# A fused low-rank update: one load in place of two, a sum moved ahead of a turn, and other waits for two stores

## The chip, the cores and the metric

The kernel runs on one core of a Trainium2 chip. The time is that of one execution on the device, in microseconds (us). The core has five engines that run side by side and meet through semaphores: TensorE (PE in the profile; PEld is its loading of weights), VectorE (DVE), ScalarE (ACT), GpSimd (POOL) and SyncE (SP), which here only issues transfers. Sixteen DMA engines move the data between the chip's memory (DRAM) and the core's SBUF; TensorE writes to PSUM.

## The reference

```python
def reference(x, A, B, scale):
    lora = np.matmul(np.matmul(x, A), B)
    return (x + scale * lora).astype(np.float32)
```

`x` is 16 x 512 x 768 in fp32, `A` is 768 x 16, `B` is 16 x 768, `scale` is 0.5. So 8192 rows of 768 numbers are read, each gets a small low-rank correction, and 8192 rows are written: 25.2 MB in, 25.2 MB out.

## The kernel before

**Tiles, parts, groups.** The 8192 rows are 64 tiles of 128 rows. A tile of fp32 is 393,216 bytes. For transfers the tiles lie in five parts of 9, 7, 16, 16 and 16 tiles (`PARTS`, L14); within a part each of the 128 partitions holds neighbouring rows, so that a partition's share of a transfer is one contiguous run. `LOADS` (L106) lists the loads as (part, first tile, tiles). The buffer `x_sb` has room for 48 tiles; the last 16 tiles reuse the places of the first 16, so the loads of part 4 wait until stores 0 and 1 are done. Results are summed in place in `x_sb` and stored from there, one store for each part (`STORES`, L128).

**Groups.** Computation goes by eight groups of 8 tiles (`GROUP`). Group g goes through these steps:

1. *narrowed* (L186): the 8 tiles are cast from fp32 to fp16 into `xn`, the first four by ScalarE, the last four by GpSimd. It waits for the load, and for `s_taken`, which says that TensorE has begun on the group before.
2. *turned* (L248): VectorE transposes all 8 tiles in blocks of 32 x 32, from `xn` to `xt`.
3. *projected* (L278): 24 matmuls form x times A in PSUM (`ps_yt`). They run in two halves of 12; the last one raises `s_y`.
4. ScalarE multiplies the result by the scale, in four instructions, and spreads it into `y_bd` (L238).
5. *raised* (L293): for each of four pairs of tiles TensorE multiplies by B, four matmuls, into one of two PSUM buffers (`lora_ps`). Raising pair p of a group needs the buffer that was last read for the pair two before it (`s_free`). The last matmul of a pair raises `s_lora`.
6. *summed* (L252): VectorE adds a pair's PSUM buffer to its two tiles in `x_sb`.

**The order on each engine is written out.** TensorE's loop (L324) does, for group g: raise pairs 0 and 1; wait for the turn of group g+1; project its first half; raise pairs 2 and 3; project the second half. VectorE (L265) does the turn of group g+1 and then the four sums of group g. ScalarE (L232) does its cast of group g+1 and then the multiplies of group g. GpSimd does its casts one after the other.

**SyncE's order** (L136). It issues the loads of parts 0 to 3 at the start, then `summed(0)`: it waits for the sums of group 1, and passes on to TensorE that the last pair's buffer is free (`s_free[3]`; VectorE signals `s_sum` there instead). Then it waits until `s_lora` counts ten pairs, that is until group 2's first two pairs are raised, and issues stores 0 and 1. When store 0 is done it issues the first load of part 4, when store 1 is done the second. Store 2 waits for the sums of group 3 and for `s_raise`, which counts the first raising matmul of each group, to reach 6. Stores 3 and 4 wait for the sums of groups 5 and 7. All transfers go through this one queue.

Of the kernel before, what the change touches and what calls it, by code (L numbers as in the profile page):

```python
# [13 lines left out]
PARTS = [9, 7, 16, 16, 16]  # L14


GROUP = 8
# [11 lines left out]
def kernel(  # L29
# [19 lines left out]
    NG = sum(PARTS) // GROUP  # L49
    PAIRS = GROUP // 2  # L50
# [32 lines left out]
    def sem(name):  # L83
        sems.append(nc.alloc_semaphore(name))
        return sems[-1]
# [10 lines left out]
    def memory(t2, i, s, n):  # L96
        S = PARTS[i]
        return t2[ds(parts[i], S * P), :].rearrange("(p s) d -> p s d", s=S)[:, ds(s, n), :]

    def held(i, s, n):  # L100
        return tiles(where.index((i, s)), n)

    def tiles(t, n):
        return x_all[:, ds(t % ROOM, n), :]

    LOADS = [  # L106
        (0, 0, 2), (0, 2, 7), (1, 0, 7), (2, 0, 8), (2, 8, 8), (3, 0, 16), (4, 0, 8), (4, 8, 8)
    ]
    s_load = [sem(f"s_load{k}") for k in range(len(LOADS))]

    def load_of(t):
        i, s = where[t]
        return next(k for k, ld in enumerate(LOADS) if ld[0] == i and ld[1] <= s < ld[1] + ld[2])
# [6 lines left out]
    s_y, s_spread, s_lora = sem("s_y"), sem("s_spread"), sem("s_lora")  # L120

    s_free = [sem(f"s_free{p}") for p in range(PAIRS)]
    s_out0, s_out1, s_raise = sem("s_out0"), sem("s_out1"), sem("s_raise")

    s_sum, s_out = sem("s_sum"), sem("s_out")

# [1 line left out]
    STORES = [(0, 0, 9), (1, 0, 7), (2, 0, 16), (3, 0, 16), (4, 0, 16)]  # L128

    STORED = [where.index((i, s + n - 1)) // GROUP for i, s, n in STORES]  # L130
    assert STORED[0] == STORED[1]

    section = ExitStack()
    section.enter_context(tc.tile_critical(no_gpsimd_drain=True))  # L134
# [1 line left out]
    def on_sync(e):  # L136
        def load(k):
            ld = LOADS[k]
            e.dma_start(out=held(*ld), in_=memory(x2, *ld)).then_inc(s_load[k], 16)  # L139

        def summed(k):
            e.wait_ge(s_sum, sorted(set(STORED)).index(STORED[k]) + 1)
            if STORED[k] + 1 < NG:

                e.sem_inc(s_free[PAIRS - 1], 1)

        def store(k, done):
            st = STORES[k]
            e.dma_start(out=memory(out2, *st), in_=held(*st)).then_inc(done, 16)

        load(0)
        load(1)
        e.wait_ge(s_ready, 1)
        blocks = A.rearrange("(c e) r -> c (e r)", e=64)
        for c in range(SETS):
            e.dma_start(
                out=a_rows[c : SET * SET : SET, :], in_=blocks[ds(c * SET, SET), :]
            ).then_inc(s_a, 16)
        e.wait_ge(s_brows, 1)
        e.dma_start(out=b_rows[0 : R * APART : APART, :], in_=B).then_inc(s_b, 16)  # L160
        for k in range(2, len(LOADS) - 2):
            load(k)

        for p in range(2, PAIRS):
            e.sem_inc(s_free[p], 1)
        summed(0)


        e.wait_ge(s_lora, 2 * PAIRS + 2)
        store(0, s_out0)  # L170
        store(1, s_out1)
        e.wait_ge(s_out0, 16)
        load(len(LOADS) - 2)
        e.wait_ge(s_out1, 16)
        load(len(LOADS) - 1)
        for k in range(2, len(STORES)):
            summed(k)
            if k == 2:


                e.wait_ge(s_raise, 6)
            store(k, s_out)

    here = set()
# [1 line left out]
    def narrowed(e, copy, g, first, n=SUB):  # L186
        t = g * GROUP + first
        for k in dict.fromkeys(load_of(t + k) for k in range(n)):
            if (e, k) not in here:
                here.add((e, k))  # L190
                e.wait_ge(s_load[k], 16)
        if g:
            e.wait_ge(s_taken, g)
        ins = copy(out=xn[:, ds(first, n), :], in_=tiles(t, n))  # L194

        ins.then_inc(s_narrow if g else s_first if first else s_a, 1)
# [30 lines left out]
    def on_scalar(e):  # L227
        narrowed(e, e.copy, 0, SUB // 2, SUB // 2)
        narrowed(e, e.copy, 0, SUB)
        e.wait_ge(s_bp, 1)  # L230
        e.copy(out=b_mm, in_=lora[0][:, 0, :]).then_inc(s_bm, 1)  # L231
        for g in range(NG):  # L232
            if g + 1 < NG:
                narrowed(e, e.copy, g + 1, 0)
            e.wait_ge(s_y, g + 1)
            for b in range(NQ):
                q = ds(b * Q, Q)
                last = e.mul(out=y_bd[q, :, q], in_=y_ps[q, :, :], mul=sc)  # L238
            last.then_inc(s_spread, 1)

    def on_vector(e):
        e.wait_ge(s_a, SETS * 16 + 1)
        e.transpose(  # L243
            out=a_t[0:Q].rearrange("i k r c -> i (k r) c"),
            in_=a_rows[0:Q].rearrange("c (i k r) -> c (k r) i", k=2, r=R),
        ).then_inc(s_ready, 1)

        def turned(first, n):  # L248
            ts = [v[:, ds(first, n), :].bitcast(fp32) for v in (xt, xn)]
            return e.transpose(out=ts[0], in_=ts[1])  # L250

        def summed(g, p):  # L252
            xs = tiles(g * GROUP + 2 * p, 2)
            e.wait_ge(s_lora, g * PAIRS + p + 1)
            ins = e.tensor_tensor(out=xs, in0=xs, in1=lora[p % 2], op=mybir.AluOpType.add)  # L255
            if p + 1 == PAIRS and g in STORED:
                ins.then_inc(s_sum, 1)
            elif g + 1 < NG or p + 2 < PAIRS:
                ins.then_inc(s_free[p], 1)

        for h in range(2):
            e.wait_ge(s_first, h + 1)
            ins = turned(h * SUB, SUB)
        ins.then_inc(s_turned, 1)
        for g in range(NG):  # L265
            if g + 1 < NG:
                e.wait_ge(s_y, g + 1)
                e.wait_ge(s_narrow, 2 * (g + 1))  # L268
                turned(0, GROUP).then_inc(s_turned, 1)
            for p in range(PAIRS):  # L270
                summed(g, p)

    def on_tensor(e):


        xv = xt.rearrange("p s (c j k) -> p s c j k", c=NC, k=2)

        def projected(first, last):  # L278
            for m in range(first, last):
                c, k = divmod(m, 2)  # L280
                mm = e.matmul(  # L281
                    y_ps, w_bd[:, c, k, :], xv[:, :, c, :, k],
                    start=(m == 0), stop=(m == MMS - 1),
                )
                if m == 0:
                    mm.then_inc(s_turned, -1)
                if m == 1:

                    mm.then_inc(s_taken, 1)
                if m == MMS - 1:  # L290
                    mm.then_inc(s_y, 1)

        def raised(p):  # L293
            if p == 0:
                e.wait_ge(s_spread, 1)
            free = s_free[(p + 2) % PAIRS]
            e.wait_ge(free, 1)
            t = lora[p % 2]
            mms = []
            for k in range(2):  # L300
                for n0, w in ((0, 512), (512, 256)) if k == 0 else ((0, 256), (256, 512)):
                    mms.append(e.matmul(  # L302
                        t[:, k, ds(n0, w)], y_bd[:, 2 * p + k, :], b_mm[:, ds(n0, w)],
                        start=True, stop=True,
                    ))
            if p == 0:
                mms[0].then_inc(s_raise, 1)
                mms[2].then_inc(s_spread, -1)
            mms[1].then_inc(free, -1)
            mms[-1].then_inc(s_lora, 1)  # L310

        e.wait_ge(s_pick, 2)
        e.wait_ge(s_bh, 1)
        for n0, w in ((0, 512), (512, 256)):
            last = e.matmul(  # L315
                lora[0][:, 0, ds(n0, w)], pick.rearrange("p b r -> p (b r)"),
                b_half[:, ds(n0, w)], start=True, stop=True,
            )
        last.then_inc(s_bp, 1)
        e.wait_ge(s_w, 1 + NQ)  # L320
        e.wait_ge(s_turned, 1)
        projected(0, MMS)
        e.wait_ge(s_bm, 1)
        with e.Fori(0, NG - 1):  # L324
            raised(0)
            raised(1)
            e.wait_ge(s_turned, 1)
            projected(0, MMS // 2)
            raised(2)
            raised(3)  # L330
            projected(MMS // 2, MMS)
        for p in range(PAIRS):
            raised(p)

    on_sync(nc.sync)
    on_gpsimd(nc.gpsimd)
    on_scalar(nc.scalar)
    on_vector(nc.vector)
    on_tensor(nc.tensor)

# [43 lines left out]
```

## Time and profile before

| | us |
|---|---|
| median of 3 runs (123.42 to 123.6) | 123.47 |
| the profiled execution | 123.43 |
| its span, first to last instruction | 121.6 |
| VectorE busy | 81.7 |
| TensorE matmuls busy | 49.8 |
| ScalarE busy | 37.4 |
| GpSimd busy | 28.4 |

How to read it: the span is cut into 40 slices of 3.04 us, with a digit for the busy share in tenths. The granted clock of TensorE stands there as well. A group of instructions is named by its line, engine, operation, and what it writes and reads. In the timeline each row has the start, the duration, the engine, the line, the count, and in brackets the idle time ahead of it with what ended it. Rows of SP give the moment of issue of a transfer, not its duration. The transfers put through 50.43 MB in 1928 packets, a mean of 415 GB/s over the span. Every sum of a pair takes 1.7 us on VectorE, every turn of a full group 3.4, every cast of four tiles 2.75 on either engine.

### The profile page before, as it was taken

How to read it: one execution, taken by the hardware profiler on the slowest of the kernel's cores; microseconds unless marked ns; L12 is line 12 of the kernel's file. 1: busy time of each engine (PE TensorE's matmuls, PEld its weight loads, DVE VectorE, ACT ScalarE, POOL GpSimd, SP SyncE). 2: the span in 40 equal slices, each digit the busy share in tenths (PEclk: the TensorE clock that was granted, in tenths of full speed). 3: DMA queues.
4: the chain of work that ended last, by engine and by line, in shares of the span. 5: the costliest groups of instructions: out<-in, count | busy, mean ns of one | idle time of the engine just before them, and what ended most of it. 6: DMA issues, size and time to landing. Idle time of an engine off the chain costs nothing.

```text
span 121.6 us, 884 instructions
## 1 busy us (share of the span) xinstructions
PE 49.8 (41%) x322; PEld 29.2 (24%) x322; DVE 81.7 (67%) x42; ACT 37.4 (31%) x43; POOL 28.4 (23%) x24
## 2 busy tenths in 40 slices
PE   0000209487457547746745734774674320000000
PEld 0000006253223424424423322442442110000000
DVE  0000970599999999999999989999995990000000
ACT  4000967626408312735340093643004000000000
POOL 7730567126009002605300080620000000000000
PEclk9999999999999999999999999999999995555555
DMA  3999999999999897999999999998999899899890
GB/s 63 437 431 457 446 398 469 404 420 469 437 517 420 356 517 336 427 421 410 446 416 436 428 428 485 420 517 372 404 517 404 372 517 404 372 517 404 372 517 0
DMA packets 1928, 50.43 MB, mean 415 GB/s; under 512 B 236, under 2 KB 236, under 8 KB 392
## 3 DMA queue, kind: packets, MB, share of 16 engines
q1 hardware_dynamic: 1928, 50.43, 97.0%
HBM read 25.26 MB, written 25.17 MB: 415 GB/s over the span
## 4 chain that ended last, share of the span: by engine, by line
DVE 33%; DMA 29%; PE 9%; ACT 6%; POOL 2%; issue 2%; SPq 0%; DVEq 0%
DVE x_sb L255 21%; DMA x_sb<-in_x_dram 20%; DVE xt L250 12%; DMA out_dram<-x_sb 9%; PE ps_yt L281 6%; ACT xn L194 3%; PE lora_ps L302 3%; ACT y_bd L238 2%; POOL xn L194 2%; SPq L139 0%; SPq L379 0%; DVEq L268 0%; SPq L134 0%
## 5 line engine op out<-in xcount | busy, mean ns | idle before, releaser
L255 DVE TENSOR_TENSOR x_sb<-x_sb,lora_ps 128x1536 f32<-128x1536 f32 x32 | 53.7, 1735 | 1.4 <-PE lora_ps L302 1.4
L194 ACT CAST xn<-x_sb 128x3072 f16<-128x3072 f32 (+1 forms) x9 | 23.4, 2609 | 35.9 <-DMA x_sb<-in_x_dram 24.8
L302 PE MATMUL lora_ps<-b_mm,y_bd 128*128 128x512 f16 (+1 forms) x128 | 25.0, 328 | 22.6 <-ACT y_bd L238 14.3
L194 POOL CAST xn<-x_sb 128x3072 f16<-128x3072 f32 (+1 forms) x8 | 20.7, 2586 | 43.9 <-DMA x_sb<-in_x_dram 24.6
L250 DVE STREAM_TRANSPOSE xt<-xn 128x3072 f32<-128x3072 f32 (+1 forms) x9 | 27.1, 3006 | 5.3 <-PE ps_yt L281 4.4
L281 PE MATMUL ps_yt<-xt,w_bd 128*128 128x256 f16 x192 | 25.2, 282 | 12.2 <-DVE xt L250 12.2
L281 PEld LDWEIGHTS ps_yt<-xt,w_bd 128*128 128x128 f16 x192 | 18.5, 99 | 19.7 <-issue 15.4
L302 PEld LDWEIGHTS lora_ps<-b_mm,y_bd 128*128 128x128 f16 x128 | 10.6, 97 | 35.5 <-ACT y_bd L238 16.6
L238 ACT ACTIVATE y_bd<-ps_yt 32x256 f16<-32x256 f32 x32 | 12.0, 374 | 18.7 <-PE ps_yt L281 18.4
L243 DVE STREAM_TRANSPOSE a_t<-a_rows 32x1024 f32<-32x1024 f32 x1 | 2.0, 1955 | 12.2 <-DMA a_rows<-in_A_dram 12.2
L315 PE MATMUL lora_ps<-b_half,pick 128*128 128x512 f16 (+1 forms) x2 | 0.8, 500 | 13.5 <-POOL b_half L212 13.5
L315 PEld LDWEIGHTS lora_ps<-b_half,pick 128*128 128x128 f16 x2 | 0.1, 105 | 13.5 <-issue 13.5
L212 POOL CAST b_half<-b_rows 128x768 f16<-128x768 f32 x1 | 0.8, 827 | 5.5 <-DMA b_rows<-in_B_dram 5.5
L220 POOL COPY w_bd<-w_one 32x384 f16<-32x384 f16 x4 | 2.0, 500 | 0.2
L194 ACT ACT_TABLE_LOAD x1 | 1.3, 1283 | 0.9 <-SPq L134 0.9
L202 POOL MEMSET w_bd<- 128x1536 f32 x1 | 1.4, 1372 | 0.0
L214 POOL CAST w_one<-a_t 32x384 f16<-32x384 f32 x1 | 0.9, 857 | 0.9 <-DVE a_t L243 0.9
L199 POOL MEMSET a_rows<- 32x1024 f32 x1 | 0.9, 941 | 0.5 <-SPq L134 0.5
L231 ACT CAST b_mm<-lora_ps 128x768 f16<-128x768 f32 x1 | 0.8, 798 | 0.0
L200 POOL MEMSET b_rows<- 128x768 f32 x1 | 0.7, 728 | 0.0
L203 POOL MEMSET y_bd<- 128x512 f32 x1 | 0.5, 514 | 0.0
L205 POOL TENSOR_SCALAR_AFFINE_SELECT pick<-pick 128x128 f16<-128x128 f16 x1 | 0.3, 298 | 0.0
(5 smaller groups left out, 0.6 us busy)
## 6 DMA issues: line engine op xcount, KB each, us to landing
out_dram<-x_sb SPq DMA_DIRECT2D x3, 6144.0 KB, 20.1
x_sb<-in_x_dram SPq DMA_DIRECT2D x4, 3072.0 KB, 17.6
x_sb<-in_x_dram SPq DMA_DIRECT2D x1, 6144.0 KB, 41.6
x_sb<-in_x_dram SPq DMA_DIRECT2D x2, 2688.0 KB, 12.4
out_dram<-x_sb SPq DMA_DIRECT2D x1, 3456.0 KB, 11.5
out_dram<-x_sb SPq DMA_DIRECT2D x1, 2688.0 KB, 17.7
x_sb<-in_x_dram SPq DMA_DIRECT2D x1, 768.0 KB, 4.5
a_rows<-in_A_dram SPq DMA_DIRECT2D x3, 16.0 KB
```

Of the source, the lines that this page charges most:

```text
L194: ins = copy(out=xn[:, ds(first, n), :], in_=tiles(t, n))
L199: e.memset(a_rows[0:Q], 0.0).then_inc(s_ready, 1)
L202: e.memset(w_bd.rearrange("p c k m -> p (c k m)").bitcast(fp32), 0.0)
L214: e.tensor_copy(out=w_one.rearrange("i (c e) k r -> i c e (k r)", c=SETS), in_=a_t[0:Q].rearrange("i k r (e c) -> i c e (k r)", c=SET)[:, ...
L220: e.tensor_copy(out=w_bd[ds(b * Q, Q), :, :, ds(b * Q, R)], in_=w_one).then_inc(s_w, 1)
L238: last = e.mul(out=y_bd[q, :, q], in_=y_ps[q, :, :], mul=sc)
L243: e.transpose(out=a_t[0:Q].rearrange("i k r c -> i (k r) c"), in_=a_rows[0:Q].rearrange("c (i k r) -> c (k r) i", k=2, r=R),).then_inc(s_r ...
L250: return e.transpose(out=ts[0], in_=ts[1])
L255: ins = e.tensor_tensor(out=xs, in0=xs, in1=lora[p % 2], op=mybir.AluOpType.add)
L281: mm = e.matmul(y_ps, w_bd[:, c, k, :], xv[:, :, c, :, k], start=(m == 0), stop=(m == MMS - 1),)
L302: mms.append(e.matmul(t[:, k, ds(n0, w)], y_bd[:, 2 * p + k, :], b_mm[:, ds(n0, w)], start=True, stop=True,))
L315: last = e.matmul(lora[0][:, 0, ds(n0, w)], pick.rearrange("p b r -> p (b r)"), b_half[:, ds(n0, w)], start=True, stop=True,)
```

## The change

Five edits, made together:

- Part 2 is loaded by one transfer of 16 tiles in place of two of 8, on one semaphore. Groups 2 and 3 both lie in part 2.
- VectorE: in the turn for group 1 it sums the first pair of group 1 ahead of turning group 2, and the other three pairs behind it. In all other groups the order is as before.
- ScalarE: for g = 1 the cast of group 2 comes behind the multiplies of group 1 and no longer ahead of them.
- SyncE: store 0 waits for the projection of group 2 (`s_y` at 3) and no longer for the sums of group 1 and ten raised pairs. Its nine tiles are group 0 and the first tile of group 1's first pair, whose sum now stands ahead of group 2's turn. Then come the wait for group 1's sums with the passing on of `s_free[3]`, and store 1.
- SyncE: store 2 waits for the projection of group 5 (`s_y` at 6) and no longer for the first raising matmul of group 5. The semaphore `s_raise` is gone.

```diff
     LOADS = [
-        (0, 0, 2), (0, 2, 7), (1, 0, 7), (2, 0, 8), (2, 8, 8), (3, 0, 16), (4, 0, 8), (4, 8, 8)
+        (0, 0, 2), (0, 2, 7), (1, 0, 7), (2, 0, 16), (3, 0, 16), (4, 0, 8), (4, 8, 8)
     ]
...
         for p in range(2, PAIRS):
             e.sem_inc(s_free[p], 1)
-        summed(0)
-        e.wait_ge(s_lora, 2 * PAIRS + 2)
+        e.wait_ge(s_y, 3)
         store(0, s_out0)
+        summed(1)
         store(1, s_out1)
...
             if k == 2:
-                e.wait_ge(s_raise, 6)
+                e.wait_ge(s_y, 6)
             store(k, s_out)
...
         for g in range(NG):
-            if g + 1 < NG:
+            if g + 1 < NG and g != 1:
                 narrowed(e, e.copy, g + 1, 0)
             e.wait_ge(s_y, g + 1)
...
             last.then_inc(s_spread, 1)
+            if g == 1:
+                narrowed(e, e.copy, g + 1, 0)
...
         for g in range(NG):
+            ahead = 1 if g == 1 else 0
+            for p in range(ahead):
+                summed(g, p)
             if g + 1 < NG:
                 e.wait_ge(s_y, g + 1)
                 e.wait_ge(s_narrow, 2 * (g + 1))
                 turned(0, GROUP).then_inc(s_turned, 1)
-            for p in range(PAIRS):
+            for p in range(ahead, PAIRS):
                 summed(g, p)
...
             if p == 0:
-                mms[0].then_inc(s_raise, 1)
                 mms[2].then_inc(s_spread, -1)
```

More of the change, by code (lines that the diff above doesn't have):

```diff
@@ L122 @@
     s_free = [sem(f"s_free{p}") for p in range(PAIRS)]
-    s_out0, s_out1, s_raise = sem("s_out0"), sem("s_out1"), sem("s_raise")
+    s_out0, s_out1 = sem("s_out0"), sem("s_out1")
     s_sum, s_out = sem("s_sum"), sem("s_out")
@@ L130 @@
     STORED = [where.index((i, s + n - 1)) // GROUP for i, s, n in STORES]
-    assert STORED[0] == STORED[1]
+    assert STORED[0] == STORED[1] == 1 and PARTS[0] <= GROUP + 2
     section = ExitStack()
```

## The prediction

> **What bounds the kernel now.** I first read the busy shares by slice on the profile's page, to see which resource is never idle, and the queue's total.
>
> ```profile
> span 121.6 us, 884 instructions
> DVE  0000970599999999999999989999995990000000
> DMA  3999999999999897999999999998999899899890
> q1 hardware_dynamic: 1928, 50.43, 97.0%
> ```
>
> The 16 DMA engines are busy from the third microsecond to the end, VectorE (DVE) nearly as much but only from 22 to 101 us. 50.43 MB must pass one queue in order of issue. A tile (393,216 bytes) costs 0.906 to 0.914 us: in the chain of waits
>
> ```profile
> 44.45 11.48 DMA out_dram<-x_sb
> 55.95 13.71 DMA x_sb<-in_x_dram
> 93.86 6.75 DVE x_sb L255 x4
> ```
>
> the second line holds what followed store 0, namely store 1 and load 6, 15 tiles in 13.71 us. The last line is the last sums: they end at 100.61. The last store goes out then, though by the trace's packet records the engines stay on store 3 until 104.76 (the first to finish) to 105.77 us (the last). Compute is therefore some 4 us ahead of the DMA at the end. So the time is the packets' own duration plus any hole in the queue, and before has no hole: at every sampled moment from 2.5 to 119 us the records show 16 packets or more in flight.
>
> Next, the timeline around the change (VectorE's turn is the transpose, L250; the sums are L255).
>
> ```profile
> 31.44 1.53 ACT L238 ACTIVATE y_bd<-ps_yt 32x256 f16<-32x256 f32 x4 [2.18 <-PE ps_yt L281]
> 32.44 3.36 DVE L250 STREAM_TRANSPOSE xt<-xn 128x3072 f32<-128x3072 f32 x1
> 33.03 1.47 PE L302 MATMUL lora_ps<-b_mm,y_bd 128*128 128x512 f16 x8 [1.62 <-ACT y_bd L238]
> 35.73 6.71 DVE L255 TENSOR_TENSOR x_sb<-x_sb,lora_ps 128x1536 f32<-128x1536 f32 x4
> 35.95 1.50 PE L281 MATMUL ps_yt<-xt,w_bd 128*128 128x256 f16 x12 [1.45 <-DVE xt L250]
> 39.17 0.82 PE L302 MATMUL lora_ps<-b_mm,y_bd 128*128 128x512 f16 x4 [0.84 <-DVE x_sb L255]
> 39.83 1.50 PE L281 MATMUL ps_yt<-xt,w_bd 128*128 128x256 f16 x12
> 44.45 0.82 SPq L149 DMA_DIRECT2D out_dram<-x_sb  x2
> 47.78 2.75 ACT L194 CAST xn<-x_sb 128x3072 f16<-128x3072 f32 x1 [4.88 <-DMA x_sb<-in_x_dram]
> 74.47 26.50 SPq L149 DMA_DIRECT2D out_dram<-x_sb  x3
> ```
>
> This is group 1 (counting from 0): turn of group 2, four sums of 1.68 us, projection of group 2 in two halves around two raisings, and the issue of stores 0 and 1 at 44.45. The cast at 47.78 marks the landing of load (3,0,16), 0.44 us behind its last packet at 47.34.
>
> Last, TensorE's rate and granted clock in chosen stretches (length, busy time and matmuls, clock, DMA).
>
> ```profile
> 18.20:19.80 1.60, 1.59 (x8) 1.00 1.00 430
> 21.40:22.50 1.10, 1.07 (x10) 1.00 0.88 380
> 31.48:34.90 3.42, 1.47 (x8) 1.00 1.15 496
> 96.34:99.75 3.41, 0.98 (x5) 1.00 0.97 418
> 99.50:100.00 0.50, 0.00 (x0) 0.75 1.59 688
> ```
>
> The same matmul starts every 0.2 us after an idle spell and every 0.11 us later; the clock row misses that first slow state. At the end the clock falls at 99.75, 1.6 us behind the last matmul.
>
> **The change, part by part.**
>
> *One load of 16 tiles for two of 8.* Each engine moves 8 packets of 49,152 bytes for 16 of 24,576. The records give 1.8175 and 0.9152 us as means: 8 x (2 x 0.9152 - 1.8175) = 0.10 us, and one completion packet of 0.009 us less. Bounds: a gain of 0.13 (16 tiles at 0.906 in place of 0.914), and none, as the bytes are the same. I take -0.11. One issue of some 0.5 us leaves SP's queue at 4.6 to 6.7 us, hidden under the loads before it. What it costs: tiles 16 to 23 no longer land at 25.5 but with tiles 24 to 31, last packet at 32.80 - 0.1, so the casts may start at 33.15 (with the 0.44).
>
> *ScalarE and GpSimd.* GpSimd's cast of group 2 moves from 26.55 to 33.15; only its next cast is behind it. ScalarE does group 1's four multiplies first (31.44 to 32.97, unmoved), then its cast: 33.15 to 35.9. Without that reordering the multiplies would have waited for the load.
>
> *VectorE's pair ahead.* After group 0's sums (32.44) VectorE waits for the first raising (33.03 + 0.82), sums pair 0 from 33.9 to 35.6, then turns group 2 behind the casts: 35.9 to 39.3 instead of 32.44 to 35.80. Pair 1 follows until 40.95. Pair 2 needs the third raising, which TensorE has queued behind the projection's first half. Warm: first half from 39.35, third raising done at 41.65, so pairs 2 and 3 end at 45.1, against 42.44: VectorE is 2.65 us late.
>
> *TensorE's clock.* It now idles from 34.50 to 39.35, 4.85 us; the longest gap before between 26 and 98 us is 2.98 (71.08 to 74.05). The row that cooled held 0.98 us of work in 3.41; the row from 31.48 held 1.47 and stayed warm. Wherever a stretch of 3.41 us is laid, one in this gap ends with under 0.98, so I expect half clock. Half clock doubles 4.2 us of work to about 7.9 (24 projection matmuls at 0.213, two raisings at 1.28). If it recovers between 40.9 and 45.1 (one to two such stretches after the fall), group 2's projection ends at 44.3 to 46.3, and VectorE is 3.2 to 4.25 us late.
>
> [...]
>
> *Store 0's new wait.* It leaves at 44.0 (warm) to 46.3 in place of 44.45, and no longer waits for the group's sums; store 1 leaves with those sums at 45.1 to 46.7 and has 8 us of store 0 ahead of it. The engines finish the loads between 46.42 and 47.23 (the recorded 46.53 and 47.34, less 0.11). A store must be issued 1.06 us (load 0: issue 0.97, first packet 2.03) to 1.28 us (store 2: 74.47 to 75.75, without a hole) ahead. An early engine's hole only eats its lead over the last, so nothing is lost up to an issue at 47.23 - 1.28 = 45.95. Most of 44.0 to 46.3 lies below; I take 44.9 and no loss. At the far end, 46.3 + 1.06 to 1.48 (load 0's first packets) + 0.05 to 0.9 (their lengthening over 0.234) gives a loss of 0.2 to 1.4. Behind store 0 on SP stands the relay that frees pair 3 to TensorE; it fires with the sums as before, and the next raising that needs it comes no earlier than 46.7.
>
> *Store 2's new wait.* Group 5's projection ended at 71.08 and will end at 73.7 to 75.3; the old wait fired at 74.47. Needed: 76.46 - 1.28 = 75.2. No loss, at the far end a few tenths. Behind it on SP wait only the relay of group 5 (84 to 87) and store 3. Dropping the counter on the raising removes an update and no instruction.
>
> *What is late next.* VectorE regains 0.38 us at 72.2 to 72.57 (it waited there for load 6) and ends at 102.9 to 104.5 for 100.61. Store 4 is needed at 105.66 - 1.28 = 104.4. The cover is just enough; if it were gone, each further microsecond would be paid in full.
>
> **Sum.** 123.43 (the profiled execution: span 121.6 and 1.83 around it) - 0.11 = 123.32; it stands 0.04 below the median 123.47, so 123.36.
>
> **Rivals.**
>
> *Slower: the halved clock holds store 0 back.* Decides from an issue after 45.95. For it: the gap of 4.85 us, and that the early matmuls needed 3.0 us of steady work (18.21 to 21.24) to speed up. Against: the lower half of the recovery times is harmless. Typical price 0.6: 123.95, at most 124.8.
>
> *Slower: store 4 comes late.* VectorE more than 3.8 us late at the end opens a hole near 105 us. For it: the margin is a few tenths in the upper case. Against: it needs nearly the whole bound. Some 0.5 over: 123.85.
>
> *The merge has no price at all.* Bytes decide, not packets, and the delays are covered: 123.47, the same side as my forecast.
>
> *Faster: a transfer has a fixed cost that is now paid once less.* Against: at the boundary near 24.7 to 25.5 us each engine starts the next load's packet 0.006 us behind the completion packet. To be seen it would need 0.25 us, more than twice my term; say 123.15.
>
> [...]
>
> **How the numbers follow.** 0.2% is 0.25 us, about what a measurement of this kernel can tell from no change. Forecast (covered, with or without the 0.11): 0.48, its own range 123.25 to 123.65. Store 0 late: 0.32. Store 4 (or store 2) late: 0.10. Faster: 0.10. So same 0.48, slower 0.42, faster 0.10. The range is 123.2 to 124.3: it leaves out half of the faster case and the last third of the bounds on a late store 0.
>
> **What would show it.** Right: casts of group 2 starting near 33.2; a sum at 33.9 ahead of the turn; TensorE idle about 4.9 us before 39.3, then matmuls at twice their time for some microseconds; stores 0 and 1 issued one by one, the first between 44.3 and 46; the last sum at 103 to 104.5; 1784 packets (128 rows and 16 completions fewer). Wrong: a DMA slice near 46 to 48, 75 to 77 or 105 to 107 us with a hole, the span longer by that hole; or loads landing earlier than by bytes.

## The result, and the profile after

The changed kernel takes 124.63 us (median of 6 runs, 124.27 to 125.13), the kernel before beside it 123.55 (123.42 to 123.60). The ratio is 1.0088, with a 95% interval of 1.0071 to 1.0105: slower by 1.1 us, where no change (123.36) was forecast, and outside the range of 123.2 to 124.3. The chain of events is that of the rival with a chance of 0.32, the halved clock that holds store 0 back. Its typical price of 0.6 us was too low, its upper end of 124.8 was not. The runs below put some 0.6 to 0.7 of the 1.1 us down to the moment of store 0; for the rest no cause is shown.

The page of the profile after: the span, three rows of the busy shares by slice, and the queue's total.

```profile
span 122.8 us, 881 instructions
DVE  0000970499869569999999999999999699200000
PEclk9999999999995589999999999999999996555555
DMA  3999999799799896999989999995995996998990
q1 hardware_dynamic: 1784, 50.43, 96.6%
```

The clock row has what before's did not: two slices at half speed, from 37 to 43 us. VectorE has a dent in the same place and ends at 105.25 us in place of 100.61. The packets are 1784, as forecast; the bytes are the same.

The timeline around the change, in the order of the prediction's own fence (sums are now L258, turns L253, projections L288).

```profile
33.33 2.75 POOL L194 CAST xn<-x_sb 128x3072 f16<-128x3072 f32 x1 [11.73 <-DMA x_sb<-in_x_dram]
33.70 2.75 ACT L194 CAST xn<-x_sb 128x3072 f16<-128x3072 f32 x1
34.59 1.75 DVE L258 TENSOR_TENSOR x_sb<-x_sb,lora_ps 128x1536 f32<-128x1536 f32 x1 [1.38 <-PE lora_ps L309]
36.55 3.38 DVE L253 STREAM_TRANSPOSE xt<-xn 128x3072 f32<-128x3072 f32 x1 [0.21 <-ACT xn L194]
40.08 2.72 PE L288 MATMUL ps_yt<-xt,w_bd 128*128 128x256 f16 x12 [4.88 <-DVE xt L253]
42.59 2.25 PE L309 MATMUL lora_ps<-b_mm,y_bd 128*128 128x512 f16 x8
44.11 3.42 DVE L258 TENSOR_TENSOR x_sb<-x_sb,lora_ps 128x1536 f32<-128x1536 f32 x2 [2.54 <-PE lora_ps L309]
44.68 1.50 PE L288 MATMUL ps_yt<-xt,w_bd 128*128 128x256 f16 x12
46.21 1.76 SPq L149 DMA_DIRECT2D out_dram<-x_sb  x2
76.20 29.40 SPq L149 DMA_DIRECT2D out_dram<-x_sb  x3
98.50 6.75 DVE L258 TENSOR_TENSOR x_sb<-x_sb,lora_ps 128x1536 f32<-128x1536 f32 x4 [1.38 <-PE lora_ps L309]
```

The reader sees the whole chain of the rival: 4.88 us without work for TensorE, then 12 matmuls in 2.72 us that take 1.50 elsewhere, VectorE waiting 2.54 us for the raising behind them, and store 0 issued at 46.21 for 44.45. VectorE's last sum ends at 105.25 for 100.61. Store 2 goes out at 76.20 for 74.47.

Where the 1.2 us of span went is told by the last engine's completion packet of each transfer, in the trace's packet records:

| last completion, us | before | after | later by |
|---|---|---|---|
| load (3,0,16) | 47.29 | 47.34 | 0.05 |
| store 0 | 55.47 | 55.52 | 0.05 |
| store 1 | 61.91 | 62.82 | 0.91 |
| load 6, load 7 | 69.24, 76.52 | 70.16, 77.43 | 0.92, 0.91 |
| store 2 | 91.02 | 92.07 | 1.05 |
| store 3, store 4 | 105.72, 120.23 | 106.89, 121.40 | 1.17 |

These times are counted from the first instruction, as the rows of the profile are. The prediction counted its packet times 0.05 us too late, so that the cast at 47.78 starts 0.49 us behind the last packet and not 0.44, and the lead of a store reads 1.23 us and not 1.28; its bound of 45.95 stays, since both of its terms shift.

There was a hole ahead of store 0 (0.38 us per engine on average), and it cost the last engine nothing, as the prediction had it for a hole that only eats an engine's lead; the first packet of store 0 came 0.86 us behind its issue, sooner than the prediction's lead of a store allowed. The loss came one transfer later, at the switch from store 1 (writing) to load 6 (reading): the last packets of store 1 took up to 1.585 us for 0.799, and the packets of store 1 together were 0.72 us per engine longer than undisturbed ones, on average, with no hole there. Before, they were 0.16 us longer (one single packet took 1.596 us there too, so the mean tells and not the longest packet). In the view by stretches (length, clock, DMA share, GB/s) it is a rate that falls while the share stays full; before, after:

```profile
60.00:63.00 3.00, 1.00 1.04 421
```

```profile
60.00:63.00 3.00, 1.00 1.10 360
```

### The profile page after: what moved, and what is told of

It reads as the page before. It is cut to its first block, busy times and chain, and to the rows that moved or that the text cites. A ratio compares the mean times of both kernels' runs of the same rounds, so it can differ in the third digit from the quotient of the medians.

```text
span 122.8 us, 881 instructions
## 1 busy us (share of the span) xinstructions
PE 52.9 (43%) x322; PEld 30.7 (25%) x322; DVE 81.9 (67%) x42; ACT 37.5 (31%) x43; POOL 28.4 (23%) x24
## 2 busy tenths in 40 slices
DMA packets 1784, 50.43 MB, mean 411 GB/s; under 512 B 220, under 2 KB 220, under 8 KB 376
## 3 DMA queue, kind: packets, MB, share of 16 engines
q1 hardware_dynamic: 1784, 50.43, 96.6%
## 4 chain that ended last, share of the span: by engine, by line
DVE 56%; PE 12%; DMA 7%; ACT 4%; issue 4%; SPq 1%; POOL 1%; POOLq 0%; DVEq 0%
DVE x_sb L258 33%; DVE xt L253 22%; PE ps_yt L288 9%; DMA a_rows<-in_A_dram 7%; PE lora_ps L309 3%; ACT xn L194 2%; ACT y_bd L238 2%; DVE a_t L246 2%; SPq L156 1%; POOL a_rows L199 1%; POOLq L385 0%; DVEq L275 0%; SPq L134 0%
## 5 line engine op out<-in xcount | busy, mean ns | idle before, releaser
L258 DVE TENSOR_TENSOR x_sb<-x_sb,lora_ps 128x1536 f32<-128x1536 f32 x32 | 53.9, 1741 | 5.3 <-PE lora_ps L309 5.3
L309 PE MATMUL lora_ps<-b_mm,y_bd 128*128 128x512 f16 (+1 forms) x128 | 26.0, 339 | 20.4 <-ACT y_bd L238 13.0
L288 PE MATMUL ps_yt<-xt,w_bd 128*128 128x256 f16 x192 | 27.5, 298 | 16.2 <-DVE xt L253 16.2
L253 DVE STREAM_TRANSPOSE xt<-xn 128x3072 f32<-128x3072 f32 (+1 forms) x9 | 27.1, 3011 | 5.7 <-PE ps_yt L288 5.5
L288 PEld LDWEIGHTS ps_yt<-xt,w_bd 128*128 128x128 f16 x192 | 19.4, 104 | 24.6 <-issue 19.4
L309 PEld LDWEIGHTS lora_ps<-b_mm,y_bd 128*128 128x128 f16 x128 | 11.1, 100 | 33.7 <-ACT y_bd L238 15.5
```

What stands on the lines that cost most here:

```text
L288: mm = e.matmul(y_ps, w_bd[:, c, k, :], xv[:, :, c, :, k], start=(m == 0), stop=(m == MMS - 1),)
L309: mms.append(e.matmul(t[:, k, ds(n0, w)], y_bd[:, 2 * p + k, :], b_mm[:, ds(n0, w)], start=True, stop=True,))
```

## The experiments

Times are medians beside runs of the kernel before on the same chip (123.52 to 123.63). What the packets did is collected behind the last run.

**The gap filled.** TensorE's loop is written out, and 32 matmuls go into the gap.

```diff
-        with e.Fori(0, NG - 1):
+        for g in range(NG - 1):
             raised(0)
             raised(1)
+            for _ in range(32 if g == 1 else 0):
+                e.matmul(spare, w_bd[:, 0, 0, :], b_mm[:, 0:256], start=True, stop=True)
             e.wait_ge(s_turned, 1)
```

> The changed kernel with TensorE's loop written out and 32 matmuls into an unused PSUM tile put between raising pair 1 of group 1 and the wait for group 2's turn (some 3.5 us of work in the gap of 4.88). The clock theory (the gap halves TensorE's clock, and the slow projection makes store 0 late): projection of group 2 at full rate, about 4.2 us from its first to its last matmul and not 6.1, store 0 issued at 44 to 45, no hole near 47 us, VectorE's last sum by 103.5, 123.4 to 123.6 in all. The load theory (the later landing of group 2 and VectorE's lateness are what costs, whatever the clock): 124.2 or more. The loop written out should cost nothing by either.

Measured: 125.30 us, ratio 1.0126 (1.0108 to 1.0145). The clock stayed full, the projection took its 1.50 us per half, store 0 went out at 43.65, and the kernel was slower than the change. By itself that spoke against the clock theory. Two things were mixed in it, as later runs showed: code that was fetched, and a store that is too early (the last packets of load (3,0,16) were 0.45 us per engine longer). The queues of this kernel:

```profile
q1 hardware_dynamic: 1784, 50.43, 95.8%
q8 instruction: 3, 0.05, 0.2%
```

**Store 0 early, in the changed kernel.**

```diff
-        e.wait_ge(s_y, 3)
+        e.wait_ge(s_taken, 3)
         store(0, s_out0)
```

> The changed kernel with one edit: store 0 waits for the second matmul of group 2's projection in place of the last one. The clock still falls. If the late store 0 is the whole loss: issued near 40.5, no hole near 47 us, 123.4 to 123.6. If VectorE's lateness of about 4 us costs by itself: the last store is issued near 105.3, the engines are free from 104.7 to 105.7, and the hole comes there: 123.8 to 124.2. If neither is the cause: 124.6 as before the edit.

Measured: 124.21 us, 1.0050 (1.0035 to 1.0065). Store 0 was issued at 40.46. The hole at 47 us and the longer packets of store 1 were gone, and yet 0.6 us stayed: now the last packets of load (3,0,16) took up to 3.01 us for 1.82, and the load completed 1.2 us later than before. The hole expected near 105 us did not come. None of the three numbers expected was for this reason.

**A late store 0 alone, in the kernel before.**

```diff
-        e.wait_ge(s_lora, 2 * PAIRS + 2)
+        e.wait_ge(s_taken, 4)
         store(0, s_out0)
```

> The kernel before with one edit: stores 0 and 1 wait for the second matmul of group 3's projection (near 46.1) in place of ten raised pairs (44.45). Loads, VectorE, ScalarE and TensorE as before. If a store 0 issued near 46.2 costs all that the change lost: 124.5 to 124.7, with store 1's last packets lengthened to about 1.6 us as in the changed kernel. If it costs only the hole that is seen near 47 us: 123.8 to 124.1. If the prediction's margin was right (harmless up to 45.95): 123.6 to 123.9.

Measured: 124.81 us, 1.0085 (1.0054 to 1.0116). In the profiled execution store 0 was issued at 46.81, 0.6 us later than in the changed kernel, with store 1 right behind it. Nothing else in the code was changed, and the clock is full until store 1 is done (it fell later, at 73.91). So a late store 0, with store 1 behind it, costs by itself as much as the change lost. The longer packets of store 1 came with it, 0.75 us per engine, and store 1 completed 1.5 us later than before. The issue, and the stretch of the fence above, for this kernel:

```profile
46.81 0.82 SPq L149 DMA_DIRECT2D out_dram<-x_sb  x2
60.00:63.00 3.00, 1.00 1.01 322
```

**The two waits alone, in the kernel before.** Store 0 at the end of group 2's projection and ahead of `summed`, store 2 at the end of group 5's; nothing else.

```diff
-        summed(0)
-        e.wait_ge(s_lora, 2 * PAIRS + 2)
+        e.wait_ge(s_y, 3)
         store(0, s_out0)
+        summed(1)
...
-                e.wait_ge(s_raise, 6)
+                e.wait_ge(s_y, 6)
```

> The kernel before with the edits to the two waits alone (store 0 at the end of group 2's projection and ahead of the sums of group 1, store 2 at the end of group 5's projection); two loads of part 2, VectorE and ScalarE as before. Clock theory: store 0 at 41.4, store 1 at 42.5, store 2 at 71.1, the time as before, 123.5. A theory that the new waits do harm by themselves: 124 or more.

Measured: 124.16 us, 1.0055 (1.0031 to 1.0079), with store 0 at 42.10 and store 2 at 71.84. The prediction's picture, in which an early store only queues up, is wrong. The last packets of the load were 0.61 us per engine longer.

**The gap filled, and the stores on a mark.** The first kernel of this section, with stores 0 and 2 on the third of ScalarE's multiplies (`if b == 2: last.then_inc(s_mark, 1)`, waits for 3 and 6).

> The kernel of the run with filled gap (full clock), with one more edit: stores 0 and 2 wait for the third of ScalarE's four multiplies of groups 2 and 5, some 1.2 us behind the end of the projection. New theory, the window: a store that is queued before the last load packets start lengthens those packets; one that comes after about 45.4 leaves a hole, and then the next switch of direction costs. By it: store 0 at 44.5 to 45.1, store 2 at 74.6 to 75.2, no lengthened packets and no hole, 123.4 to 123.7. Theory that the merged load, the loop written out or the added matmuls cost by themselves: 124.8 or more, as without the edit.

Measured: 125.64 us, 1.0168 (1.0152 to 1.0185). Store 0 was at 44.90, as wished, and 15 engines finished the load by 47.14. The sixteenth finished at 48.75. A piece of code of 16 KB had held it for 1.10 us from 37.53 us on; its next packet took 2.28 us for 1.82, its last one 2.41. That pointed at the written-out code.

**Early by one wait less, and by one raised pair, in the kernel before.**

```diff
-        e.wait_ge(s_lora, 2 * PAIRS + 2)
```

> The kernel before without the wait for ten raised pairs: stores 0 and 1 go out with the sums of group 1, near 42.5 in place of 44.45. Nothing else changed. Window theory: the last packets of load (3,0,16) take 2.3 to 2.8 us in place of 1.82, it lands 0.5 to 0.7 later, 124.1 to 124.4. Rival, the prediction's own assumption: an early store only queues up, 123.5 to 123.7.

```diff
-        e.wait_ge(s_lora, 2 * PAIRS + 2)
+        e.wait_ge(s_lora, 2 * PAIRS + 1)
```

> The kernel before with stores 0 and 1 waiting for nine raised pairs in place of ten: issue near 43.75, 0.7 us earlier. Window theory: the first packets of a store come 0.9 to 1.3 us behind its issue, so at 44.7 to 45.1, while the last load packets start at 44.7 to 45.5: a part of the engines is hit, 123.7 to 124.1. Rival, early is harmless: 123.5 to 123.7.

Measured: early 124.00 us, 1.0033 (1.0022 to 1.0043), store 0 at 41.95, the load's last packets 0.72 us per engine longer. One pair earlier 123.58 us, 1.0002 (0.9993 to 1.0011). In the profiled execution, whose computing started late, store 0 went out at 44.35, and the load's last packets were undisturbed. So there is a stretch without a loss, which holds 44.35 and 44.45, with a cost on either side. How wide it is the traces don't show: at 43.65, in the run with the gap filled, the load's packets were already longer. In the kernel before, 2.5 us earlier cost 0.42 us.

**Are engines in step what pays?** The late kernel, with one more load of 8 rows of 16 KB ahead of store 0, which keeps half of the engines busy longer.

> The kernel with the late stores 0 and 1 (second matmul of group 3's projection), and ahead of store 0 one more load of 8 rows of 16 KB into unused SBUF, which keeps 8 of the 16 engines busy 0.6 us longer, so that the engines are out of step again behind the hole. Theory that engines in step pay for the switch from store 1 to load 6: the last packets of store 1 lengthen by less than half of the 0.7 us per engine seen without the extra load. Rival, the lengthening comes with the late issue whatever the step of the engines: 0.7 again.

Measured: 126.26 us in two runs (1.0219, 1.0173 to 1.0266). The longer packets of store 1 fell from 0.75 to 0.42 us per engine; the first eight engines to arrive paid, the later eight did not. That is near the line that was drawn (half) and doesn't settle it, as the extra load also moved everything behind it.

**Other waits in the changed kernel.**

```diff
-        e.wait_ge(s_y, 3)
+        e.wait_ge(s_lora, 2 * PAIRS)
...
-                e.wait_ge(s_y, 6)
+                e.wait_ge(s_lora, 5 * PAIRS)
```

> The changed kernel with other waits for stores 0 and 2: the eighth and the twentieth raised pair (groups 0 and 1, groups 0 to 4), so the end of the raising that stands ahead of the projection's second half. The clock still falls. Store 0 near 44.2 to 44.9, store 2 near 74.2 to 74.9, both where the kernel before has them. If the moment of store 0 is all that the change lost: 123.4 to 123.6. If VectorE's lateness costs too: a hole ahead of the last store near 105 to 106, 123.7 to 124.1. If the merged load costs by itself: 124.2 or more.

Measured: 123.89 us (123.59 to 124.81), 1.0041 (1.0019 to 1.0063). Store 0 at 44.59, store 2 at 74.71, the clock still halved, VectorE still late. The moment of store 0 gave back 0.74 of the 1.08 us. By the ratios it is 0.58, since the runs fall into two groups: eight from 123.59 to 124.20, four from 124.56 to 124.81, as slow as the change. In the profiled execution (124.20) the hole ahead of the last store did come, on 12 of the 16 engines, up to 0.96 us. But the engine that finished last had none: store 4 took 14.50 us there.

**The gap filled, with the loop kept.** TensorE's loop stays a loop, turned round so that it begins at the wait for the turn; the 32 matmuls are a loop of one matmul, stores 0 and 2 on the second multiply.

> The changed kernel with the gap filled by 32 matmuls as before, but with TensorE's loop kept as a loop (turned round, so that it begins at the wait for the turn, with its first pass written out and the added matmuls in a loop of their own), and stores 0 and 2 on the second of ScalarE's four multiplies of groups 2 and 5. If the two runs with the gap filled were slow because the loop written out has to be fetched as 16 KB pieces of code through the DMA engines: no instruction queue among the DMA queues, full clock, store 0 near 44.7, VectorE's last sum by 103.3, 123.35 to 123.6. If the filling itself, or the merged load, costs: 124.5 or more again.

Measured: 131.63 us. The small loop took far longer than its matmuls:

```profile
34.93 11.23 PE L346 MATMUL spare_ps<-b_mm,w_bd 128*128 128x256 f16 x32
```

A turn with one matmul in it costs 0.35 us (11.23 / 32; from 35.69 us on the loads of weights are 0.38 us apart), so the projection came at 46.24 and store 0 at 52.98. So few matmuls did not keep the clock up either: it was halved from 39.74 to 49.98 us. And one piece of code was fetched all the same (`q8 instruction: 1, 0.02, 0.0%`). The run shows nothing on the theories, except that a hole of 7 us is followed by the same 0.74 us per engine at store 1.

**The loop written out, alone.** The kernel before with `for _ in range(NG - 1)` in place of `e.Fori(0, NG - 1)`.

> The kernel before with TensorE's loop written out seven times, nothing else. If fetching code through the DMA engines makes one engine late: an instruction queue with about three packets of 16 KB, one or two engines behind the others by 1.5 to 2 us, 124.8 to 125.6. If writing it out is free: 123.5 to 123.7.

Measured: 124.40 us, 1.0061 (1.0042 to 1.0080). Less than expected, but clear; one engine finished load (3,0,16) at 48.29, the others by 47.21. A piece of code had held the late one for 1.07 us from 41.27 us on.

```profile
q8 instruction: 2, 0.03, 0.1%
```

**The gap filled in a branch.** This is the clean form: the loop stays, and one pass takes a branch with eight turns of four matmuls.

```diff
         with e.Fori(0, NG - 1) as g:
             raised(0)
             raised(1)
+            with e.If(g == 1):
+                with e.Fori(0, 8):
+                    for _ in range(4):
+                        e.matmul(spare, w_bd[:, 0, 0, :], b_mm[:, 0:256], start=True, stop=True)
             e.wait_ge(s_turned, 1)
...
+                if b == 1:
+                    last.then_inc(s_mark, 1)
...
-        e.wait_ge(s_y, 3)
+        e.wait_ge(s_mark, 3)
```

(Store 2 waits for `s_mark` at 6.)

> The changed kernel with the gap of group 1 filled by eight turns of a small loop of four matmuls into unused PSUM (in a branch that only the pass for group 1 takes; the loop of TensorE stays a loop, so no code to fetch), and stores 0 and 2 on the second of ScalarE's four multiplies of groups 2 and 5. Clock theory: full clock through the gap, group 2's projection in 4.2 us and not 6.1, VectorE's last sum by 103.5 in place of 105.3, store 0 at 44.3 to 45.1 and store 2 at 74.4 to 75.2: the whole loss is gone, 123.35 to 123.6. If the lateness of VectorE was not what remained in the run with other waits: 123.9 again. If the merged load costs by itself: 124.2 or more.

Measured: 123.99 us, 1.0031 (1.0020 to 1.0042). The mechanics came as expected:

```profile
34.15 3.66 PE L339 MATMUL spare_ps<-b_mm,w_bd 128*128 128x256 f16 x32
39.70 1.50 PE L291 MATMUL ps_yt<-xt,w_bd 128*128 128x256 f16 x12 [1.89 <-DVE xt L256]
44.65 1.09 SPq L150 DMA_DIRECT2D out_dram<-x_sb  x2
```

The clock is full, no code was fetched (q1 is the only queue, with 1784 packets), VectorE's last sum ends at 103.02, store 2 is at 74.76. The time was 0.43 us above before all the same. So the halved clock explains why store 0 was late, but with the clock cured and store 0 put back by the mark 0.4 us of the loss stay.

**The merged load undone alone.** The changed kernel with `(2, 0, 8), (2, 8, 8)` in `LOADS`.

> The changed kernel with part 2 loaded by two transfers of 8 tiles again; VectorE's pair ahead, ScalarE's order and the two waits stay. If the later landing of the merged load is what makes store 0 late: group 2 is cast by 35.7 at the latest, but its turn still waits for the pair ahead (35.6), so TensorE's gap stays near 4.4 us and the clock falls; store 0 near 45 to 46, 124.2 to 124.7, hardly better than the change. If the merged load is the cause by itself: 123.5 to 123.7.

Measured: 124.13 us, 1.0054 (1.0041 to 1.0068), 0.5 us better than the change. Yet TensorE's gap is the same to the hundredth:

```profile
33.22 2.75 ACT L194 CAST xn<-x_sb 128x3072 f16<-128x3072 f32 x1
36.08 3.38 DVE L253 STREAM_TRANSPOSE xt<-xn 128x3072 f32<-128x3072 f32 x1 [0.21 <-ACT xn L194]
39.60 2.72 PE L288 MATMUL ps_yt<-xt,w_bd 128*128 128x256 f16 x12 [4.88 <-DVE xt L253]
45.11 1.88 SPq L149 DMA_DIRECT2D out_dram<-x_sb  x2
```

The turn waits for ScalarE's cast, which stands behind the four multiplies, whether the tiles landed at 25.5 or at 33. So the gap comes from the reordering on ScalarE and VectorE, not from the load. What gave back the 0.5 us is not shown by this run: in its profiled execution, the fastest of the six, store 0 also went out 1.1 us earlier than in the changed kernel's. The computing had started earlier there, and the clock was halved for 3.41 us (39.02 to 42.43) in place of 6.83 (37.36 to 44.19).

**Load 6 later, in the kernel before.**

```diff
         e.wait_ge(s_out0, 16)
+        e.wait_ge(s_lora, 4 * PAIRS)
         load(len(LOADS) - 2)
```

> The kernel before with one more wait: the first load of part 4 also waits for the sixteenth raised pair (near 59.8), so it goes out 3.9 us later, still ahead of the end of store 1 (61.2 to 62.0). Theory that a transfer of the other direction which is queued before the last packets start lengthens them, at any switch: store 1's last packets take 0.80 us again (0.17 us per engine longer before), 123.3 to 123.5. Rival, that lengthening has nothing to do with the moment of issue: 123.5 to 123.6; with a hole near 61 to 62, 123.7 to 124.

Measured: 124.87 us (123.69 to 125.16), 1.0082 (1.0054 to 1.0109). Half of the theory came true: with the load issued at 60.89 the packets of store 1 were 0.01 us per engine longer instead of 0.16. That fits longer packets that come from a load queued behind them; but a queued load is not enough for them, since the runs with an early store had one too and no longer packets of store 1. And the load arrived too late: 15 of the 16 engines stood idle ahead of it, 0.62 us per engine on average, and its first packets took up to 2.41 us, 0.70 us per engine more. The time expected for the theory was a miss; a hole near 61 to 62 us was the rival's, with a price that was too low.

**Stores 0 and 1 together, in the kernel with the branch.** `summed(1)` stands ahead of store 0 again, and store 2 is on the third multiply.

> The run with the branch and the small loop (full clock) with stores 0 and 1 going out together behind the sums of group 1 (near 45.2 and 45.6, where the kernel before has 44.45 and 44.9) and store 2 on the third multiply of group 5 (near 75.1). If what was left there (0.4 us) came from store 1 and store 2 reaching the queue at another moment than before: 123.4 to 123.65. If it is the price of the merged load or of VectorE's 2.65 us: 123.9 to 124.1 again.

Measured: 124.37 us (124.01 to 125.08), 1.0073 (1.0049 to 1.0097), with store 0 at 45.39. Neither number. The 0.4 us are not cured by putting the stores side by side.

**One transfer more.** Part 3 as `(3, 0, 8), (3, 8, 8)`, in the kernel before and in the kernel with the branch.

> The kernel before with part 3 loaded by two transfers of 8 tiles in place of one of 16; nothing else. In the runs so far the packets at the switch from store 1 to load 6 are 0.16 to 0.26 us per engine longer where part 2 comes as two loads, and 0.41 to 0.45 where it comes as one. Theory that one transfer more ahead of the stores shortens this: 0.1 or less, 123.3 to 123.5. Theory that the size of part 2's load alone decides, or chance: 0.16 to 0.26 again, 123.5 to 123.7 (with 0.1 us more for the smaller packets).

> The run with the branch and the small loop (full clock, store 0 near 44.7), with part 2 in one load as there and part 3 in two: as many transfers ahead of the stores as in the kernel before. Theory that the number of transfers ahead of the stores decides how long the packets at the switch are: 0.16 to 0.26 us per engine, 123.55 to 123.75. Rival, that it is something else in the changed kernel (VectorE's 2.65 us, part 2's load): 0.41 to 0.45 again, 123.9 to 124.1.

Measured: in the kernel before 123.77 us, 1.0015 (1.0003 to 1.0026); the packets of store 1 were 0.19 us per engine longer, so no gain. In the changed one 123.87 us (123.49 to 124.55), 1.0028 (1.0011 to 1.0044); there 0.20 us instead of 0.44. In the changed kernel the packets went as the count of transfers would have it; in the kernel before one transfer more shortened nothing. The time gained 0.1 us at most, within the two intervals. This stays open.

**What the packets did.** From the packet records: by how much the last packets of load (3,0,16), those of store 1 and the first of load 6 are longer than an undisturbed packet, and the hole ahead of store 0, in us per engine.

| kernel | store 0 issued | load longer | hole | store 1 longer | load 6 longer | that execution | median |
|---|---|---|---|---|---|---|---|
| changed, store 0 early | 40.46 | 0.97 | 0 | 0.01 | 0 | 124.23 | 124.21 |
| before, one wait less | 41.95 | 0.72 | 0.05 | 0.01 | 0.01 | 124.17 | 124.00 |
| before, the two waits alone | 42.10 | 0.61 | 0 | 0.01 | 0 | 123.94 | 124.16 |
| before, one pair earlier | 44.35 | 0.02 | 0 | 0.26 | 0.07 | 123.42 | 123.58 |
| before | 44.45 | 0.01 | 0 | 0.16 | 0.02 | 123.43 | 123.55 |
| branch, part 3 in two loads | 44.49 | 0.01 | 0 | 0.20 | 0.07 | 123.68 | 123.87 |
| changed, other waits | 44.59 | 0.02 | 0 | 0.45 | 0.12 | 124.20 | 123.89 |
| branch | 44.65 | 0.02 | 0.01 | 0.44 | 0.11 | 124.26 | 123.99 |
| before, part 3 in two loads | 45.04 | 0.01 | 0 | 0.19 | 0.02 | 123.83 | 123.77 |
| changed, part 2 in two loads | 45.11 | 0.01 | 0 | 0.25 | 0.07 | 123.81 | 124.13 |
| branch, stores together | 45.39 | 0.02 | 0 | 0.41 | 0.13 | 124.05 | 124.37 |
| changed | 46.21 | 0.02 | 0.38 | 0.72 | 0.14 | 124.75 | 124.63 |
| before, late store 0 | 46.81 | 0.01 | 0.89 | 0.75 | 0.12 | 125.14 | 124.81 |

The issue, the packets and the time before the last are of one execution, so they belong together; the median is of all runs. Where the longer packets add up to 0.35 us per engine or less, the execution took 123.42 to 123.83 us; where they add up to 0.56 or more, 123.94 to 125.14. An early store 0 (40.46 to 42.10) lengthened the load's last packets by 0.61 to 0.97 us per engine, and then store 1 passed undisturbed (0.01); a late one (46.21 and 46.81) left a hole of 0.38 and 0.89, and then store 1's packets were 0.72 and 0.75 longer. In between stands a stretch in which the first are undisturbed and the second longer by 0.16 to 0.26 us in the rows with two loads of part 2, and by 0.41 to 0.45 in those with one, save the row with part 3 in two. Why the two exclude each other, and whether the merged load raises the second, was not settled: each row is a single execution.

## Why the prediction was wrong, step by step

- **The merged load, -0.11.** As a transfer it came as priced: from the landing of load (1,0,7) to that of part 2, on the middle engine, 14.53 us instead of 7.31 + 7.30, so -0.08. Whether it costs elsewhere stays open. Undone alone it gave back 0.5 us, but store 0 went out earlier there as well. With store 0 back at its old moment (other waits, the branch) 0.4 us stayed, and that may be the merged load or VectorE's 2.65 us: no run has the merged load without the rest. No rival had these 0.4 us.
- **ScalarE and GpSimd.** GpSimd's cast came at 33.33 (33.15 expected). ScalarE's came at 33.70, held by its multiplies. The sentence that the casts "may start at 33.15" made the load the cause of the late turn. It is one of two, and they come within half a microsecond of each other: in the run with the branch ScalarE's cast did wait for the load (until 33.29), with two loads of part 2 it started at 33.22 behind the multiplies.
- **VectorE's pair ahead.** 34.59, 36.55 and 39.86 where 33.9, 35.9 and 39.3 were forecast. The 0.65 us is the start: ScalarE's multiplies behind the first projection began at 23.20 for 22.51, since its 24 matmuls took 5.28 us for 4.26; the record of full clock begins at 23.70 us in that execution and at 21.24 in that of before. This is luck: the first projection took over 5 us in nine of the nineteen profiled executions, and 4.1 to 4.7 in the others, of which before's is one. It moves all of the computing against the loads. Whether it makes the wide spread of the change's runs is not shown, since one of them has a trace.
- **TensorE's clock.** Right. A gap of 4.88 us (4.85), half clock (0.50) from 37.36 us on, within it, the first half of the projection in 2.72 us. (The terms given for the slow work, 24 x 0.213 and two of 1.28, make 7.7 us and not 7.9.) The stretch of 3.41 us that the forecast went by is found in the clock's own times: in the kernel before it was full for 78.51 us (21.24 to 99.75), in the changed one full for 13.65, halved for 6.83 and full for 58.03, which are 23, 4, 2 and 17 times 3.413. But it fell with more work than the 0.98 us of the row that cooled: the 3.41 us up to the fall at 37.36 held 1.25 us of matmuls, and no run shows where a limit lies. Nor does the length of the gap alone decide: near 72 us a gap of 2.98 us left the clock up in the kernel before, and one of 2.52 us halved it at 74.01 in the run with store 0 one pair earlier.
- **Store 0's new wait: the step that failed.** 46.21 lies in the forecast stretch of 44.3 to 46.3, but "I take 44.9 and no loss" took its lower half. That it came so near the upper end was luck in part: 0.65 us are the late start, and the clock stayed halved for 6.83 us, where it did for 3.41 in the three other profiles with the same gap. The issue in the change's other five runs is not recorded. And the price of a late store was wrong in kind: "an early engine's hole only eats its lead over the last, so nothing is lost". The lead was eaten (store 0 completes within 0.22 us on all engines, 0.79 before) and store 0 itself completed only 0.05 us later. But then the next switch of direction cost 0.72 us per engine in place of 0.16, which the trace of before showed in small and I did not look for. The rival's "typical price 0.6, at most 124.8" held the measured 124.63; the range was cut at 124.3. The run with the late store 0 alone shows this price without the rest of the change. That a store issued early costs 0.4 us as well stood in no step.
- **Store 2.** 76.20 for "73.7 to 75.3": late by the start and by VectorE's lateness. From load 7 to store 2 the delay grew by 0.14 us.
- **What is late next.** VectorE's last sum at 105.25, beyond the 104.5 that was allowed for; the engines were 1.2 us late themselves by then, so store 4 met no hole on any engine (14.51 us on the last).

## What to carry to other kernels

In the kernel before, whose DMA queue shows no hole, the moment at which a store reaches it had two edges: 2.5 us earlier cost 0.4 us and 2.4 us later 1.1 (by the ratio), with nothing else changed. So a wait that looks as if it held a store back for nothing is to be moved only with the packets' durations in view, before and at the next switch, and not by holes alone. And an edit that reorders work in front of a matmul group is to be checked for the idle time that it gives TensorE, since the halved clock here delayed the projection, for which store 0 waits: behind a gap of 4.88 us it took 6.10 us from its first to its last matmul, against 4.13 with the gap filled in a branch.

## What the runs showed of the hardware that was not expected

- At a switch between reading and writing the last packets of the earlier transfer took up to twice their time (1.585 us for 0.799 in store 1 of the changed kernel; 3.01 for 1.82 in load (3,0,16) with store 0 early) with no hole at that switch. From 60 to 63 us the busy share of the DMA engines read 1.04 before, 1.10 in the changed kernel and 1.01 with the late store 0 alone, and shows nothing; the rate (421 GB/s, 360 and 322) and the single packets do.
- A loop of TensorE written out seven times was fetched through the same DMA engines: two pieces of 16 KB, one engine 1.1 us behind the others, 0.84 us in all (124.40 against 123.56).
- A turn of a loop on TensorE with a single matmul of 256 columns took 0.35 to 0.38 us; with four it was 0.46 (3.66 / 8), which is the time of the four matmuls alone at 0.11 us each.
